# Fourteen modulation blocks beside channel mixing: from narrow TensorE products to sums on VectorE

## The chip, the core and the metric

The kernel runs on one core of one Trainium2 chip. The metric is the device time of one execution in microseconds; the time before is the median of three runs. The engines are named as in the profile: PE is TensorE (PEld its weight loads), DVE is VectorE, ACT is ScalarE, POOL is GpSimd, SP is SyncE, whose queue issues nearly all transfers.

## The reference

Two layers, each with token mixing and channel mixing, run over 512 latent and 256 context tokens of width 1024. Both parts of a layer are modulated: a conditioning vector, one for the latent tokens and one for the context, is multiplied by a large matrix, which gives six rows of 1024 per layer and stream (shift, scale and gate, twice).

```python
sc = silu(c)
sc_ctx = silu(c_ctx)
for l in range(DEPTH):
    last = l == DEPTH - 1
    mod_l = (sc @ w_mod[l] + b_mod[l]).reshape(Bsz, N_MOD, 1, D)
    mod_c = (sc_ctx @ w_mod[l] + b_mod[l]).reshape(N_MOD, 1, 1, D)
    ...
    hl = layer_norm(xl) * (1.0 + mod_l[:, 1]) + mod_l[:, 0]
    ...
    xl = layer_norm(DEEPNORM_ALPHA * xl + mod_l[:, 2] * yl, ln1_g[l], ln1_b[l])
    hl = layer_norm(xl) * (1.0 + mod_l[:, 4]) + mod_l[:, 3]
    xl = layer_norm(DEEPNORM_ALPHA * xl + mod_l[:, 5] * swiglu(hl, w_up[l], w_down[l]), ln2_g[l], ln2_b[l])
    ...
```

Where lines are left out stand the token mixing (RG-LRU scans, spatial gating and Fourier mixing, from which `yl` comes) and the same for the context in layer 0; in layer 1 the context only feeds the scans.

## The kernel before

All large products are done in three passes of a split format: a weight or an activation is kept as a high part (rounded on ACT by a copy) and a low part (the difference, by a subtraction on DVE or POOL), and `mm` multiplies high by high, high by low and low by high. Line 134 is the one place from which every product is issued, and line 203 (`tt`) the one place of plain additions, subtractions and products of two operands, so the profile is read by tile names: `mm` and `aux` are PSUM tiles (three of two banks, two of one bank), `f` and `r` are pieces of one large arena in SBUF, `cst` holds the identity matrix of the transposes.

Weights are "units", listed by `plan` in the order of their use. `pump` reads ahead into free arena space as long as a reserve (`self.reserve`) stays free, on SP's queue; `use` takes the next unit, splits it if it wasn't split, and splits up to `self.ahead` of the units behind it (three in channel mixing).

Token mixing of a layer (`mixing`) follows a string, `STEPS[l]`, one letter a step: `z` a Fourier input projection, `c` the first Fourier product of two token tiles, `p` the preparation of an RG-LRU scan (tanh and exp on ACT), `s` one direction of a scan, `V` and `U` the loading of the gating weights, `v` and `u` the gating projections, `g` a gate projection, `t` the gating, `L` the release of the GELUs, which before it are held back (`self.hold`: the projection is copied out of PSUM, the GELU comes later), `D` the switch of the weights' low halves from POOL to DVE (`wsub`), `m` a modulation block, `R` the gate rows. In this part the order of the products on PE is that of the string.

Channel mixing (`mlp`) runs over 22 blocks of 128 hidden columns in five groups, numbered from 0. A step projects gate and up halves of a block (`up_block`: 96 products in layer 0 and, with 512 columns, 48 in layer 1), multiplies them (L1172 on ACT, L1173 on DVE) and splits the result. At the end of a group, one step late, `project` makes the down products for every token tile, DVE multiplies them with the gate row (L1158) and POOL adds them to the residual.

Beside it the modulation is made, for which `mlp_mods` names a step: blocks 10 and 11 (the gate of channel mixing) of the layer itself at steps 1 and 2, and in layer 0 ten blocks for layer 1 at the steps of `NEXT_AT`: fourteen in all. A block is 512 columns of `w_mod`. `mod_block` makes eight products: the conditioning vectors stand as two columns of a 32-column stationary operand (`stc`), the piece of `w_mod` streams through, and four such products stand side by side in the array. `mod_part` copies the result to SBUF on ACT (L515). One step later it is finished in one of two ways. `mod_put`: four transposes, a short reduction over the four column groups, and the bias, into `modT`. `mod_rows`, for gates: the part is split, and a product with a selector matrix (`sel`) sums the four groups and spreads a row over all partitions, two products per stream, added to the bias rows.

## Time and profile before

| | |
|---|---|
| median of three runs | 1538.25 us (1536.52 to 1541.06) |
| the profiled execution | 1537.34 us |
| its span, first to last instruction | 1535.3 us |
| mean granted clock of TensorE | 0.976 of full |
| PE busy | 1443.5 us, 94% |
| DVE busy | 785.1 us, 51% |
| ACT busy | 553.6 us, 36% |
| POOL busy | 288.0 us, 19% |

Busy is the share of the whole span; the stages differ, so a stretch is read by its own window. "Idle before" is the time in which an engine had nothing to do ahead of an instruction, with the instruction that ended it. In an order of time several instructions of the same kind in a row are merged, with their count behind an x.

Layer 0's channel mixing begins at about 355 us and its last down products end at about 930, where layer 1's first projections are already under way; layer 1's channel mixing begins at about 1167 and runs to the end.

### The profile page before, as it was taken

How to read it: one execution, taken by the hardware profiler on the slowest of the kernel's cores; microseconds unless marked ns; L12 is line 12 of the kernel's file. 1: busy time of each engine (PE TensorE's matmuls, PEld its weight loads, DVE VectorE, ACT ScalarE, POOL GpSimd, SP SyncE). 2: the span in 40 equal slices, each digit the busy share in tenths (PEclk: the TensorE clock that was granted, in tenths of full speed). 3: DMA queues.
4: the chain of work that ended last, by engine and by line, in shares of the span. 5: the costliest groups of instructions: out<-in, count | busy, mean ns of one | idle time of the engine just before them, and what ended most of it. 6: DMA issues, size and time to landing. Idle time of an engine off the chain costs nothing. (4 is left out here: it accounts for less than half of the span.)

```text
span 1535.3 us, 19073 instructions
## 1 busy us (share of the span) xinstructions
PE 1443.5 (94%) x7735; PEld 1195.7 (78%) x7735; DVE 785.1 (51%) x1206; ACT 553.6 (36%) x803; POOL 288.0 (19%) x187
## 2 busy tenths in 40 slices
PE   6999888999999999999999998959898999999997
PEld 3788747788888888888888878757777788888885
DVE  6649857774323322332314386688775452543327
ACT  4576445344202202212203245786535331322210
POOL 3303312230030030030030045212320021020201
PEclk9999999999999999999999999979999999999999
DMA  9403475126106235153117104004518241442101
GB/s 322 136 15 97 131 234 183 38 88 215 42 21 213 68 100 174 55 174 106 52 46 230 41 1 123 15 30 144 176 34 241 83 136 60 127 117 67 57 14 56
DMA packets 169432, 163.59 MB, mean 107 GB/s; under 512 B 10456, under 2 KB 126648, under 8 KB 169344
## 3 DMA queue, kind: packets, MB, share of 16 engines
q1 hardware_dynamic: 169232, 162.08, 33.9%
q8 instruction: 61, 1.00, 0.3%
q0 software_dynamic: 112, 0.30, 0.1%
q14 instruction: 27, 0.22, 0.0%
HBM read 160.25 MB, written 2.10 MB: 106 GB/s over the span
## 5 line engine op out<-in xcount | busy, mean ns | idle before, releaser
L134 PE MATMUL mm<-r,r 128*128 128x512 f32 (+1 forms) x6192 | 1232.6, 360 | 23.0 <-POOL r L203 7.5
L134 PEld LDWEIGHTS mm<-r,r 128*128 128x128 f32 x6192 | 1033.6, 190 | 218.4 <-DVE f L1158 11.7
L208 ACT ACTIVATE r<-f 128x1024 fp32r<-128x1024 f32 (+3 forms) x257 | 227.3, 909 | 611.3 <-PE mm L134 324.3
L203 DVE TENSOR_TENSOR r<-f,r 128x1024 fp32r<-128x1024 f32 (+3 forms) x261 | 270.7, 1065 | 191.0 <-ACT r L208 159.5
L203 POOL TENSOR_TENSOR f<-f,f 128x1024 f32<-128x1024 f32 (+2 forms) x44 | 106.3, 2416 | 681.2 <-DVE f L1158 638.0
L1173 DVE TENSOR_TENSOR f<-mm,f 128x768 f32<-128x768 f32 (+1 forms) x44 | 36.3, 824 | 265.8 <-PE mm L134 259.4
L1158 DVE TENSOR_TENSOR f<-mm,f 128x512 f32<-128x512 f32 (+1 forms) x80 | 76.1, 952 | 158.9 <-PE mm L134 158.6
L203 POOL TENSOR_TENSOR r<-f,r 128x512 fp32r<-128x512 f32 (+2 forms) x56 | 101.5, 1820 | 209.4 <-ACT r L208 142.8
L134 PE MATMUL aux<-r,r 128*128 128x256 f32 (+1 forms) x780 | 109.7, 301 | 24.8 <-DVE r L820 9.9
L134 PEld LDWEIGHTS aux<-r,r 128*128 128x128 f32 x780 | 103.6, 206 | 33.0 <-DVE r L820 12.0
L232 POOL TENSOR_TENSOR smalls<-smalls,neghalf 128x1 f32<-128x1 f32 (+2 forms) x69 | 68.1, 988 | 289.1 <-DVE smalls L231 284.7
L203 DVE TENSOR_TENSOR f<-f,f 128x512 f32<-128x512 f32 (+1 forms) x66 | 60.6, 920 | 11.1 <-ACT f L743 8.3
L1172 ACT ACTIVATE f<-mm 128x768 f32<-128x768 f32 (+1 forms) x44 | 30.6, 696 | 96.2 <-PE mm L134 96.2
L134 PE MATMUL aux<-cst,f 128*128 128x128 f32 (+1 forms) x243 | 37.1, 283 | 24.5 <-DVE f L339 7.3
L601 ACT ACTIVATE f<-aux,modT 128x128 f32<-128x128 f32 x128 | 48.6, 467 | 29.0 <-PE aux L134 29.0
L134 PEld LDWEIGHTS aux<-cst,f 128*128 128x128 f32 (+1 forms) x243 | 28.0, 143 | 36.8 <-ACT f L586 10.2
L586 ACT ACTIVATE f<-f,smalls 128x1024 f32<-128x1024 f32 x19 | 23.6, 1242 | 91.6 <-DVE smalls L585 91.6
L134 PE MATMUL aux<-f,stc 128*32 128x512 f32 x384 | 51.0, 631 | 1.3 <-ACT f L601 1.3
L719 DVE SCALAR_TENSOR_TENSOR f<-mm,par,f 128x255 f32<-128x255 f32 (+3 forms) x48 | 26.1, 606 | 16.2 <-ACT f L713 16.2
L565 DVE BATCH_NORM_STATS2 smalls<-f 128x6 f32<-128x512 f32 x44 | 28.4, 682 | 5.9 <-DMA f<-in_ctx_dram 5.6
L743 ACT ACTIVATE f<-mm,par 128x768 f32<-128x768 f32 x32 | 28.0, 902 | 5.0 <-PE mm L134 3.7
L134 PEld LDWEIGHTS aux<-f,stc 128*32 128x32 f32 x384 | 10.4, 113 | 23.8 <-issue 18.6
(107 smaller groups left out, 612.9 us busy)
## 6 DMA issues: line engine op xcount, KB each, us to landing
f<-in_w_mod_dram SPq DMA_DIRECT2D x96, 512.0 KB
f<-in_w_up_dram SPq DMA_DIRECT2D x88, 512.0 KB
f<-in_w_down_dram SPq DMA_DIRECT2D x40, 512.0 KB
f<-in_w_in_dram SPq DMA_DIRECT2D x28, 512.0 KB
f<-in_w_out_dram SPq DMA_DIRECT2D x16, 512.0 KB
f<-in_b_mod_dram SPq DMA_DIRECT2D x6, 512.0 KB
f<-in_x_dram SPq DMA_DIRECT2D x4, 512.0 KB
f<-in_k_cosl_dram SPq DMA_DIRECT2D x4, 512.0 KB
```

Source lines behind the costliest of these rows:

```text
L134: i = f(*args, **kw)
L203: return eng.tensor_tensor(out=out, in0=a, in1=b, op=op)
L208: i = self.nc.scalar.activation(h, src, AF.Copy)
L232: self.nc.gpsimd.tensor_tensor(out=out, in0=v, in1=self.neghalf[:, 0:n], op=ALU.pow)
L565: nc.vector.bn_stats(out=st[:, c, :], in_=x[:, c * 512 : (c + 1) * 512])
L586: nc.scalar.activation(n.f, x, AF.Identity, bias=nm, scale=r)
L601: nc.scalar.activation(y.f[:, q * P : (q + 1) * P], ps[:, q * P : (q + 1) * P], AF.Identity, bias=self.modT[:, slot, k, s : s + 1], scale= ...
L719: nc.vector.scalar_tensor_tensor(out=o, in0=ps[:, i0 : i0 + o1 - o0], scalar=w(k), in1=o, op0=ALU.mult, op1=ALU.add)
L743: insts.append(nc.scalar.activation(g.f, ps[:, 256:1024], AF.Sigmoid, bias=par[:, col : col + 1]))
L1158: self.nc.vector.tensor_tensor(out=tb.f, in0=ps[:, c], in1=m[:, c], op=ALU.mult)
L1172: nc.scalar.activation(g.f, pg[:, 256 + lo : 1024], AF.Silu)
L1173: nc.vector.tensor_tensor(out=g.f, in0=pu[:, 256 + lo : 1024], in1=g.f, op=ALU.mult)
```

## The change

The fourteen blocks beside channel mixing no longer use `mod_block`. `mod_sum` adds them up on DVE: for each of the eight 128-row pieces of `w_mod`, the conditioning value of that row (a scalar per partition) times the piece, into an accumulator of 128 x 512, one per stream. Each partition then holds a partial sum of its own. `mod_cols` transposes the accumulator on PE (four transposes per stream) and reduces along the free axis on DVE; `mod_gate` splits the accumulator and multiplies it with an all-ones matrix (`onesr`), which sums over partitions and spreads the row. `mod_streams` says how many streams there are: two for layer 0's own blocks and for blocks 0 to 3 of layer 1, one for the rest. A block now spans two steps, two of its four units in each, and the list of loads is in that order. The arena reserve in channel mixing is 6000 columns instead of 5000. Both step strings are changed too: in layer 0 `D` moves from in front of `R` to in front of the last `m`; in layer 1 the first `c` moves ahead of `spp`, and `L` from in front of it to behind `U`. The blocks made inside token mixing stay as they were.

```diff
--- before.py
+++ after.py
@@ -46,7 +46,7 @@
 BETWEEN = 2
 START_RESERVE = 11000
 MIX_RESERVE = (12000, 9000)
-STEPS = ("feaekZeeppzssz6ssgpgpsssVvvsvUuuumgmcLccw7DRmtgmmm", "faeekeeZpsspszzsppLcVcssvsvgUuDsugwgtg")
+STEPS = ("feaekZeeppzssz6ssgpgpsssVvvsvUuuumgmcLccw7RmtgmmDm", "faeekeeZpsspszzcsppVcssvsvgULuDsugwgtg")
 PARAMS_AT = 5
 NEXT_AT = {6: 0, 7: 2, 9: 1, 10: 3, 12: 6, 13: 7, 15: 8, 16: 9, 18: 4, 19: 5}
 
@@ -304,6 +304,7 @@
         nc.vector.memset(self.ones, 1.0)
         self.smalls = cp.tile([P, 24 * 24], F32, tag="smalls", name="smalls")
         self.sel = cp.tile([P, 2, P], F32R, tag="sel", name="sel")
+        self.onesr = cp.tile([P, P], F32R, tag="onesr", name="onesr")
 
         self.Xb = [self.buf(D) for _ in range(NT)]
         self.X = [b.f for b in self.Xb]
@@ -349,6 +350,7 @@
         sl = self.buf(2 * P)
         nc.sync.dma_start(out=sl.f, in_=t["k_sel"])
         nc.vector.tensor_copy(self.sel.rearrange("p s n -> p (s n)"), sl.f)
+        nc.vector.tensor_copy(self.onesr, self.ones)
         sl.free()
 
     def load_tokens(self):
@@ -491,7 +493,12 @@
         at = {1: [(l, 10)], 2: [(l, 11)]}
         if l == 0:
             at.update({f: [(1, blk)] for f, blk in NEXT_AT.items()})
-        return at
+        halves = {}
+        for f, mods in at.items():
+            for m, blk in mods:
+                for i in range(2):
+                    halves.setdefault(f + i, []).append((m, blk, i))
+        return halves
 
     def mod_block(self, l, blk):
 
@@ -546,6 +553,57 @@
             o = out[s][:, hf * 512 : (hf + 1) * 512]
             nc.vector.tensor_tensor(out=o, in0=p2, in1=o, op=ALU.add)
         b.free()
+
+    def mod_streams(self, m, blk):
+
+        return 2 if m == 0 or blk < 4 else 1
+
+    def mod_sum(self, m, blk, q, acc):
+
+        nc = self.nc
+        u = self.use(f"mod{m}.{blk}.{q}")
+        for kk in range(2):
+            k = 2 * q + kk
+            w = u.low.f[:, kk * 512 : (kk + 1) * 512]
+            for s, b in enumerate(acc):
+                c = self.stc[:, k, s : s + 1]
+                if k == 0:
+                    nc.vector.tensor_scalar(out=b.f, in0=w, scalar1=c, scalar2=None, op0=ALU.mult)
+                else:
+                    nc.vector.scalar_tensor_tensor(out=b.f, in0=w, scalar=c, in1=b.f, op0=ALU.mult, op1=ALU.add)
+        self.drop(u)
+
+    def mod_cols(self, m, blk, acc):
+
+        nc = self.nc
+        j, hf = blk // 2, blk % 2
+        slot = {0: 0, 1: 1, 3: 2, 4: 3}[j]
+        red = self.small(8).rearrange("p (s k) -> p s k", k=4)
+        for s, b in enumerate(acc):
+            ps = self.psum_aux()
+            for q in range(4):
+                self.pe.transpose(ps[:, q * P : (q + 1) * P], b.f[:, q * P : (q + 1) * P], self.ident)
+            b.free()
+            nc.vector.tensor_reduce(out=red[:, s, :], in_=ps.rearrange("p (k c) -> p k c", c=P), axis=AX.X, op=ALU.add)
+            nc.vector.scalar_tensor_tensor(
+                out=self.modT[:, slot, hf * 4 : hf * 4 + 4, s], in0=red[:, s, :], scalar=(1.0 if j in (1, 4) else 0.0),
+                in1=self.par[:, j * 8 + hf * 4 : j * 8 + hf * 4 + 4], op0=ALU.add, op1=ALU.add,
+            )
+
+    def mod_gate(self, acc, hf, out):
+
+        nc = self.nc
+        for s, a in enumerate(acc):
+            b = self.buf(1024)
+            h, lo = b.r[:, 0:512], b.r[:, 512:1024]
+            self.split(h, lo, a.f)
+            a.free()
+            p2 = self.psum_aux()
+            self.pe.matmul(p2, self.onesr, h, start=True, stop=False)
+            self.pe.matmul(p2, self.onesr, lo, start=False, stop=True)
+            o = out[s][:, hf * 512 : (hf + 1) * 512]
+            nc.vector.tensor_tensor(out=o, in0=p2, in1=o, op=ALU.add)
+            b.free()
 
     def bcast_row(self, out, src):
         self.nc.sync.dma_start(out=out, in_=src.partition_broadcast(P))
@@ -1181,27 +1239,33 @@
         last = l == DEPTH - 1
         tiles = list(range(NC_T, NT)) if last else list(range(NT))
         lo = 256 if last else 0
-        self.reserve, self.owe, self.ahead, self.weng = 5000, 1, 3, "act"
-        groups, parts, rows = FF_GROUPS, {}, None
+        self.reserve, self.owe, self.ahead, self.weng = 6000, 1, 3, "act"
+        groups, parts, rows, ready = FF_GROUPS, {}, None, []
         m5b, m5 = self.gate_rows(l, 5, not last)
         hq = {}
         nxt = 0
         for gi, (f0, f1) in enumerate(groups):
             while nxt < min(f1 + 1, NFF):
                 hq[nxt] = self.up_block(l, nxt, lo, [first.pop(0) for _ in range(min(2, len(first)))])
-                for m, blk in list(parts):
-                    b = parts.pop((m, blk))
+                for m, blk in ready:
+                    acc = parts.pop((m, blk))
                     if m == l:
-                        self.mod_rows(b, blk % 2, m5, not last)
+                        self.mod_gate(acc, blk % 2, m5)
                     elif blk in (4, 5):
                         rows = rows or self.gate_rows(m, 2, False)
-                        self.mod_rows(b, blk % 2, rows[1], False)
+                        self.mod_gate(acc, blk % 2, rows[1])
                     else:
-                        self.mod_put(m, blk, b)
+                        self.mod_cols(m, blk, acc)
+                ready = []
                 if nxt == PARAMS_AT and not last:
                     self.params(1)
-                for m, blk in self.mlp_mods(l).get(nxt, ()):
-                    parts[m, blk] = self.mod_part(m, blk)
+                for m, blk, i in self.mlp_mods(l).get(nxt, ()):
+                    if i == 0:
+                        parts[m, blk] = [self.buf(512) for _ in range(1 if last else self.mod_streams(m, blk))]
+                    else:
+                        ready.append((m, blk))
+                    for q in (2 * i, 2 * i + 1):
+                        self.mod_sum(m, blk, q, parts[m, blk])
                 nxt += 1
             final = gi == len(groups) - 1
             if final:
@@ -1246,8 +1310,8 @@
         def dma(src, pat, **kw):
             return lambda b: nc.sync.dma_start(out=b.rearrange(pat, **kw), in_=src)
 
-        def mod(l, blk):
-            for q in range(4):
+        def mod(l, blk, qs=range(4)):
+            for q in qs:
                 src = t["w_mod"][l][q * 256 : (q + 1) * 256, blk * 512 : (blk + 1) * 512].rearrange("(k p) n -> p k n", p=P)
                 us.append(Unit(f"mod{l}.{blk}.{q}", 1024, dma(src, "p (k n) -> p k n", n=512), raw=True))
 
@@ -1368,8 +1432,8 @@
                     up(l, nxt)
                     if l == 0 and nxt == PARAMS_AT:
                         params(1)
-                    for m, blk in self.mlp_mods(l).get(nxt, ()):
-                        mod(m, blk)
+                    for m, blk, i in self.mlp_mods(l).get(nxt, ()):
+                        mod(m, blk, (2 * i, 2 * i + 1))
                     nxt += 1
                 down(l, gi, f0, f1)
         self.units = us
```

## Rows read from the trace of the kernel before

**Rows 1.** The page, table of engines: busy us, share of the span, instructions.
```profile
PE 1443.5 (94%) x7735; PEld 1195.7 (78%) x7735; DVE 785.1 (51%) x1206; ACT 553.6 (36%) x803; POOL 288.0 (19%) x187
```

**Rows 2.** Windows: stretch, length, busy PE, PEld, DVE, ACT, POOL (instructions), clock, DMA share.
```profile
384.00:870.00 486.00, 486.00 (x2670) 406.30 (x2669) 144.60 (x165) 98.72 (x116) 59.60 (x26) 1.00 0.34 104
...
1001.70:1021.10 19.40, 3.69 (x14) 2.79 (x13) 18.45 (x23) 19.07 (x25) 0.00 (x0) 0.57 0.13 39
1021.10:1053.00 31.90, 31.77 (x228) 30.51 (x229) 26.25 (x67) 21.76 (x28) 9.91 (x5) 0.94 0.22 68
1200.00:1500.00 300.00, 300.00 (x1325) 248.35 (x1324) 116.66 (x110) 73.26 (x92) 41.74 (x16) 1.00 0.27 81
```

**Rows 3.** Groups of instructions, 384 to 870 us: busy us, mean ns, idle before.
```profile
L134 PE MATMUL mm<-r,r 128*128 128x512 f32 (+1 forms) x2449 | 462.2, 350 | 0.0
...
L203 POOL TENSOR_TENSOR f<-f,f 128x1024 f32<-128x1024 f32 x24 | 58.3, 2429 | 402.4 <-DVE f L1158 395.3 <-DMA f<-in_w_mod_dram 4.2 <-issue 3.0
...
L134 PE MATMUL aux<-f,stc 128*32 128x512 f32 x176 | 21.2, 598 | 0.0
```

**Rows 4.** Order of time, 460 to 560 us, PE's lines: start us, length us, what.
```profile
495.69 1.92 PE L134 MATMUL aux<-f,stc 128*32 128x512 f32 x16
...
497.54 16.96 PE L134 MATMUL mm<-r,r 128*128 128x256 f32 x96
...
514.34 0.60 PE L134 MATMUL aux<-cst,f 128*128 128x128 f32 x4
...
514.87 1.92 PE L134 MATMUL aux<-f,stc 128*32 128x512 f32 x16
...
533.50 0.60 PE L134 MATMUL aux<-cst,f 128*128 128x128 f32 x4
...
533.86 26.36 PE L134 MATMUL mm<-r,r 128*128 128x512 f32 x115
```

**Rows 5.** The chain that ended last, in order of time: start, length, what.
```profile
1165.13 1.91 PE aux L134 x2
...
1167.98 1.17 PE aux L134 x8
...
1183.09 0.99 PE aux L134 x6
...
1195.20 2.32 PE aux L134 x18
```

**Rows 6.** Groups of DVE instructions by form, whole span.
```profile
L203 DVE TENSOR_TENSOR f<-f,f 128x512 f32<-128x512 f32 x45 | 35.1, 782 | 0.7
...
L379 DVE SCALAR_TENSOR_TENSOR f<-f,f 128x512 f32<-128x512 f32 x4 | 2.7, 671 | 0.0
```

**Rows 7.** Order of time, 1034 to 1040 us, POOL and DVE.
```profile
1035.94 2.40 POOL L203 TENSOR_TENSOR r<-f,r 128x1024 fp32r<-128x1024 f32 x1 [9.39 <-ACT r L208]
...
1036.02 2.87 DVE L203 TENSOR_TENSOR f<-f,f 128x512 f32<-128x512 f32 x1
```

**Rows 8.** Order of time, 798 to 832 us, SP's queue, ACT and PE.
```profile
801.79 1.45 SPq L1247 DMA_DIRECT2D f<-in_w_up_dram  x2
...
808.85 1.06 ACT L208 ACTIVATE r<-f 128x1024 fp32r<-128x1024 f32 x1 [42.78 <-DMA f<-in_w_up_dram]
...
823.88 16.96 PE L134 MATMUL mm<-r,r 128*128 128x256 f32 x96
```

**Rows 9.** Order of time, 1012 to 1022 us, PE, ACT and DVE.
```profile
1012.46 1.86 PE L134 MATMUL aux<-r,r 128*128 128x256 f32 x7 [0.46 <-DVE r L820]
...
1019.10 0.69 DVE L203 TENSOR_TENSOR f<-f,f 128x512 f32<-128x512 f32 x1
...
1019.75 1.05 ACT L819 ACTIVATE r<-aux 128x512 fp32r<-128x512 f32 x2
1020.35 1.29 DVE L820 TENSOR_TENSOR r<-aux,r 128x512 fp32r<-128x512 f32 x2 [0.56 <-ACT r L819]
...
1021.10 15.18 PE L134 MATMUL aux<-r,r 128*128 128x256 f32 x108 [6.77 <-DVE r L820]
```

## The prediction, made before the change was run

> **What bounds the kernel now.** The page's table of engines comes first: TensorE (PE) is busy 94% of the span, VectorE (DVE) 51% [rows 1]. That average covers stages with different limits, so the windows come next. In the channel mixing of layer 0 (384 to 870 us) PE is busy 486.00 of 486.00 us at granted clock 1.00 and DVE 144.60; from 1200 to 1500 us, layer 1, it is 300.00 of 300.00 against 116.66 [rows 2]. The groups of instructions of that first window say the same from the other side: the big products had 0.0 us of idle time in front of them [rows 3]. So there every microsecond that leaves PE comes off the end, provided nothing else becomes late, and DVE has 341 us to spare. Layer 1's token mixing is different: from 1001.7 to 1021.1 us PE does 3.69 us of work in 19.40 at a mean clock of 0.57, while DVE and ACT are nearly full [rows 2]. The change edits both kinds of place.
>
> **Part 1: the products that leave PE.** A block is eight products against 32 columns, recorded as 16 instructions, busy 1.92 us. What it costs the stage is start to start. A block behind a projection runs from 495.69 to 497.54, 1.85 us; one behind the four transposes of an earlier block costs more, because those transposes to the next product take 0.36 us without a block (533.50 to 533.86) and 0.53 with one (514.34 to 514.87), so 1.85 + 0.17 = 2.02 [rows 4]. Twelve of the 14 blocks lie in layer 0's channel mixing, half of them behind transposes or the like: 6 x 1.85 + 6 x 2.02 = 23.2 us. In layer 1 the second block is 2.32 us of the chain that ended last, of which I take 1.85 (the rest is two gate products that stay). The first is split in three on that chain, 1.91 + 1.17 + 0.99 us [rows 5]; the 1.91 stands where the last token tile is still being modulated, so without it PE may only wait: 2.2 to 4.1 us, and I take the 2.2. Sum removed: 23.2 + 1.85 + 2.2 = 27.2 us.
>
> **Part 2: what PE gets.** The four layer-1 blocks 0 to 3 keep two accumulators (latent and context), each transposed by itself: eight transposes instead of four, 4 x 0.36 = 1.4 us. The others keep four transposes, and the gate rows keep two products per stream, with the all-ones matrix in place of the selector. Net on PE: 27.2 - 1.4 = 25.8 us.
>
> **Part 3: what DVE gets.** Eight instructions per block and stream over 128 x 512: layer 0's two blocks and layer 1's blocks 0 to 3 have two streams, the other eight one, so 20 x 8 = 160 instructions. No row shows this form with its column scalar; the same operation over 512 SBUF elements with a constant takes 0.67 us, and the additions of that shape average 0.78, waits for GpSimd included [rows 6]. I take 0.69: 160 x 0.69 = 110 us, 99 of it in layer 0 (144 instructions); by the two rows 107 to 125. It goes into 341 us of DVE idle time there, and the 11 us of layer 1 into 183. Twelve full-width reductions replace eight short ones, some 7 us more, hidden likewise. ACT loses 14 evacuations and gains two splits: not on the path. Locally it is tighter. At steps 2, 7 and 10 two half blocks meet: 16 x 0.69 = 11 us, beside DVE's own 144.6 / 486 x 17.0 = 5.1 us in a step of 17.0 us (96 products in 16.96 us [rows 4]). That is 16 of 17; what queues behind the sums is the product of gate and up halves, the low half of that result, and the low halves of weights. The down products of a group need that result one whole step later and weights are split up to three units ahead, so a lag of some microseconds reaches nobody. I cost it at nothing, with up to 8 us for the range.
>
> **GpSimd beside it.** The trace has a DVE addition of 512 elements, two SBUF inputs, that took 2.87 us [rows 7] where another took 0.69 [rows 9]; it ended 0.55 us after a GpSimd subtraction that had started 0.08 us before it. 140 of the 160 new instructions (all but the first of each stream) have two SBUF tensor inputs, and GpSimd's residual additions (2.4 us, 24 of them in layer 0's window [rows 3]) lie in the same stage. If each of the 24 stops a sum for its whole length, DVE loses 24 x 2.43 = 58 us: 145 + 99 + 7 + 58 = 309 of 486. Still covered.
> The Trainium skill (SBUF — State Buffer, § Who interferes with whom) states this as a rule: the engines share one port pair under an exclusive lock, and a VectorE instruction with two SBUF inputs blocks, or is blocked by, a GpSimd instruction that reads SBUF. The row above agrees; by the rule the new sums are the worst kind beside GpSimd work, and the sum changes only if DVE becomes late, which is the second rival.
>
> **Part 4: loads and space.** The w_mod transfers are the same, on SP's queue, but a block's four pieces now come two per step, so at the down products of group 3 two pieces instead of four stand before the weights of step 19. That was the tightest place I found: those weights are issued at 801.79, converted on ACT from 808.85 and used at 823.88 [rows 8], 11 us to spare. Against that, the accumulators hold 512 to 1024 columns (2048 at step 2) and the reserve grows by 1000, about one weight block less read ahead. Nothing either way; a transfer into a freed w_mod buffer now waits for DVE instead of PE, with SP's later loads behind it.
>
> **Part 5: the two step strings.** Layer 0's "D" moves behind three modulation steps: one weight (the last gate column block) has its low half computed on GpSimd instead of DVE: 0, within 1 us. Layer 1 matters more. The first Fourier column step moves from behind the two scan preparations ("p") to directly behind its inputs, and "L", which releases the GELUs, behind the last gate and the loading of u. In the trace PE ends the first column step at 1012.46 + 1.86 = 1014.3, but its evacuation starts on ACT at 1019.75, behind tanh and exp of the preparations, and PE resumes at 1021.10 [rows 9]: 6.8 us. With the evacuation ahead of them PE should resume at about 1015, a gain of 5 to 6.8. After that PE is busy 31.77 of 31.90 us [rows 2], so the gain travels some way; but DVE is busy 18.45 of the 19.40 us and its scans are only put later. Later GELUs save table switches and delay the normalisation before the gating. Bounds: a loss of 2.4 (the scans finish late by the evacuations now ahead of them, 1.05 us on ACT and 1.29 on DVE [rows 9], and nothing is won) to a gain of 9 (the 6.8, and an estimated 2 us for the low clock, 0.57 over the stall [rows 2]). I take 4.
>
> **Sum.** 25.8 + 4 = 29.8 us. The profiled execution is 1537.34 us (span 1535.3), 0.9 below the median of the three timed runs, 1538.25. Forecast on the median: 1538.25 - 29.8 = 1508.5 us, 1.9% less.
>
> **The rivals.**
> First, the step strings give nothing or cost up to 2.4 us while channel mixing gives all: 1538.25 - 25.8 = 1512.5, up to 1514.9. For it: DVE and ACT are nearly full in the stall [rows 2], so the work may only be reordered. Against: the evacuation waits 5.4 us for an engine, not for data. 0.18.
> Second, DVE is late often enough to stop PE in the crowded steps and at the starts of the down groups: a third to two thirds of the gain is given back, 1516 to 1530. For it: 16 of 17 us at three steps, and the GpSimd lock. Against: the average, 52% of the window without the lock. 0.11.
> Third, slower. DVE works in order; a sum whose w_mod piece has not landed, or that GpSimd holds, stands in front of the low halves of the weights, and PE waits for those. There are 28 half blocks; one lock costs 2.87 - 0.69 = 2.18 us; if every one reached PE, 28 x 2.18 = 61 us, and 1508.5 + 61 = 1569.5. It decides from 29.8 / 28 = 1.06 us per half block, not hidden. For it: the 2.87 us row. Against: weights are converted steps ahead, PE had no wait at all in this stage, and the lock can be met only while GpSimd is active, some 60 us of 486. 0.05.
> Fourth, the change moves no time: if PE's seemingly full rows hid another limit of the stage (the loads), the gain would be under 4.6 us, about 1536. DMA is busy 0.34 of the window [rows 2] and the products show no wait for it. 0.03.
>
> **How the numbers follow.** The forecast has 0.63. The range: its fast end is full gain of part 5 and the whole first block of layer 1, 1508.5 - 5 - 1.9 = 1501.6, so 1501; its slow end takes in the first rival and about half of the second, 1522. About 1 or 2 in 10 is left out. A measurement here can tell 0.3%, 4.6 us, from no change: faster takes the forecast and the first two rivals, 0.92; same 0.03; slower 0.05.
>
> **What would show it.** In the profile after: no 32-column products after 384 us (160 records instead of 384); some 160 new DVE instructions of 0.6 to 0.8 us in two new lines, DVE at about 900 us busy; PE still without idle time in channel mixing; a step there of 17 us and the transposes, where a block stood between; the stall before 1021 shorter by some 6 us. Layer 0's channel mixing should be 21 to 23 us shorter. Wrong would be PE idle time behind DVE or ACT in channel mixing, new sums far above 0.8 us, or token mixing of layer 1 longer than before.

## The result, and the profile after the change

The changed kernel takes 1517.6 us (median of four runs, 1516.55 to 1519.18) against 1537.4 for the kernel before in the same comparison: the ratio is 0.987, with an interval of 0.9847 to 0.9895. That is 19.8 us less. The forecast was 29.8 us less, 1508.5; the time lies in the range, near its slow end. It lies in the span of times of the second rival (1516 to 1530), though what that rival names, PE stopped in the crowded steps, is not seen in layer 0's channel mixing (below).

The page of the profile after, its table of engines (busy us, share of the span, instructions), answers to [rows 1]:

```profile
span 1515.3 us, 18862 instructions
...
PE 1417.1 (94%) x7527; PEld 1197.1 (79%) x7527; DVE 896.8 (59%) x1376; ACT 548.2 (36%) x792; POOL 289.8 (19%) x188
```

PE loses 26.4 us of busy time and DVE gains 111.7. The same window as in [rows 2], 384 to 870 us (PE, PEld, DVE, ACT, POOL, clock):

```profile
384.00:870.00 486.00, 486.00 (x2606) 420.90 (x2605) 237.92 (x303) 96.44 (x108) 62.17 (x25) 1.00 0.34 105
```

The groups of DVE instructions by form over the whole span (busy us, mean ns, idle before), for the two new lines and for a line of the first one's form that was there before:

```profile
L573 DVE SCALAR_TENSOR_TENSOR f<-f,stc,f 128x512 f32<-128x512 f32 x140 | 102.4, 764 | 2.2 <-DMA f<-in_w_mod_dram 0.4
...
L571 DVE TENSOR_SCALAR f<-f,stc 128x512 f32<-128x512 f32 x20 | 9.4, 484 | 12.4 <-PE mm L134 9.9 <-POOL f L203 2.3 <-DMA f<-in_w_mod_dram 0.2
...
L678 DVE SCALAR_TENSOR_TENSOR f<-f,smalls,f 128x512 f32<-128x512 f32 x8 | 5.6, 744 | 0.0
```

PE is as full as before, at full clock; the 160 new instructions cost 102.4 + 9.4 = 111.8 us. (Line numbers behind the new functions are some 58 higher than before.)

Where the 20 us went is seen by cutting the span at marks that both traces have. On PE's order of time (start us, length us, what, idle before and what ended it) these are: a, the transposes of the last token tile in layer 0's token mixing; b, the first transposes at the end of its channel mixing; c, the products of the Fourier maps; d, the products with `ones`; e and f, the first and the last transposes at the end of layer 1's token mixing. Before:

```profile
349.82 1.09 PE L134 MATMUL aux<-cst,f 128*128 128x128 f32 x8 [0.78 <-ACT f L586]
...
960.33 1.05 PE L134 MATMUL aux<-f,cst 128*128 128x128 f32 x8
...
1083.13 1.84 PE L134 MATMUL aux<-ones,f 128*128 128x1 f32 x8 [3.24 <-DVE f L203]
...
1129.81 1.09 PE L134 MATMUL aux<-cst,f 128*128 128x128 f32 x8 [0.35 <-ACT f L586]
...
1162.17 0.66 PE L134 MATMUL aux<-cst,f 128*128 128x128 f32 x4 [2.28 <-ACT f L586]
```

and after:

```profile
353.22 1.95 PE L134 MATMUL aux<-cst,f 128*128 128x128 f32 x8 [2.22 <-ACT f L644]
...
879.42 1.09 PE L134 MATMUL aux<-cst,f 128*128 128x128 f32 x8
...
939.97 1.06 PE L134 MATMUL aux<-f,cst 128*128 128x128 f32 x8
...
1061.33 1.02 PE L134 MATMUL aux<-ones,f 128*128 128x1 f32 x8 [2.97 <-DVE f L203]
...
1105.84 1.04 PE L134 MATMUL aux<-cst,f 128*128 128x128 f32 x8
...
1144.48 1.97 PE L134 MATMUL aux<-cst,f 128*128 128x128 f32 x8 [6.60 <-ACT f L644]
```

b was at 897.48 us before. The stretches in us, worked out from these starts, with two experiments told of below (their starts read in the same view):

| stretch | before | after | both old strings | old strings, own sums held |
|---|---|---|---|---|
| start to a: layer 0 token mixing | 349.8 | 353.2 | 353.3 | 352.0 |
| a to b: layer 0 channel mixing | 547.7 | 526.2 | 524.6 | 524.6 |
| b to c | 62.9 | 60.6 | 63.3 | 60.5 |
| c to d: Fourier steps, scans, gating | 122.8 | 121.4 | 118.1 | 117.7 |
| d to e | 46.7 | 44.5 | 46.6 | 46.1 |
| e to f: last token tiles | 32.4 | 38.6 | 35.7 | 31.7 |
| f to the end: layer 1 channel mixing | 373.1 | 370.8 | 369.6 | 369.7 |
| span | 1535.3 | 1515.3 | 1511.2 | 1502.3 |

So layer 0's channel mixing gained 21.5 us, layer 1's 2.3, the three stretches from b to e 5.9 together, and two places lost: the start by 3.4 and e to f by 6.2. From b to f, layer 1's token mixing, it is 265.1 us against 264.7: no gain is left there, and the prediction had named that part growing longer as a sign of being wrong.

These are single executions, and chance is not small in them. A kernel of the experiments below, without the sums of layer 1's own blocks, has the same instructions as the changed kernel in the same order on PE, DVE, ACT and POOL up to 1127 us; its stretches are 354.0, 524.6, 63.2, 122.4 and 45.7 us, so one stretch differs by up to 2.7 us and e comes 4.1 us later. The difference in a to b has a visible source: over the 20 us from a the granted clock was 0.91 in the changed kernel and 1.00 in the other and with the old strings, behind waits of 2.22, 2.26 and 2.23 us. So the verdicts below go by the medians, and a stretch counts only where several traces agree or a wait in it explains the difference.

### The profile page after: what moved, and what is told of

Same layout as the page of the kernel before. It is cut to its first block, busy times and chain, and to the rows that moved or that the text cites. A ratio compares the mean times of both kernels' runs of the same rounds, so it can differ in the third digit from the quotient of the medians.

```text
span 1515.3 us, 18862 instructions
## 1 busy us (share of the span) xinstructions
PE 1417.1 (94%) x7527; PEld 1197.1 (79%) x7527; DVE 896.8 (59%) x1376; ACT 548.2 (36%) x792; POOL 289.8 (19%) x188
## 4 chain that ended last, share of the span: by engine, by line
PE 73%; DVE 13%; ACT 5%; issue 4%; POOL 4%; DMA 2%; SPq 0%; DVEq 0%; POOLq 0%; ACTq 0%
PE mm L134 68%; PE aux L134 5%; POOL smalls L232 2%; DVE r L203 1%; DVE f L203 1%; DVE f L678 1%; POOL r L203 1%; DVE f L1216 1%; ACT r L208 1%; DMA f<-in_b_mod_dram 1%; DVE smalls L709 1%; DVE f L835 1%; DVE f L832 1%; DVE f L1008 1%; DVE f L573 0%
## 5 line engine op out<-in xcount | busy, mean ns | idle before, releaser
L208 ACT ACTIVATE r<-f 128x1024 fp32r<-128x1024 f32 (+3 forms) x259 | 229.1, 907 | 601.6 <-PE mm L134 324.8
L203 DVE TENSOR_TENSOR r<-f,r 128x1024 fp32r<-128x1024 f32 (+4 forms) x262 | 269.7, 1053 | 140.7 <-ACT r L208 116.6
L1216 DVE TENSOR_TENSOR f<-mm,f 128x512 f32<-128x512 f32 (+1 forms) x80 | 76.2, 953 | 150.5 <-PE mm L134 146.8
L573 DVE SCALAR_TENSOR_TENSOR f<-f,stc,f 128x512 f32<-128x512 f32 x140 | 102.4, 764 | 2.2 <-DMA f<-in_w_mod_dram 0.4
L134 PE MATMUL aux<-cst,f 128*128 128x128 f32 (+2 forms) x259 | 39.0, 286 | 29.3 <-ACT f L644 13.4
L134 PEld LDWEIGHTS aux<-cst,f 128*128 128x128 f32 (+2 forms) x259 | 30.6, 145 | 40.4 <-ACT f L644 15.8
L623 DVE BATCH_NORM_STATS2 smalls<-f 128x6 f32<-128x512 f32 x44 | 28.5, 683 | 5.3 <-DMA f<-in_ctx_dram 5.0
L709 DVE BATCH_NORM_STATS2 smalls<-f 128x6 f32<-128x512 f32 x40 | 27.7, 691 | 0.5
```

The costliest lines, as they stand in the source:

```text
L134: i = f(*args, **kw)
L203: return eng.tensor_tensor(out=out, in0=a, in1=b, op=op)
L208: i = self.nc.scalar.activation(h, src, AF.Copy)
L573: nc.vector.scalar_tensor_tensor(out=b.f, in0=w, scalar=c, in1=b.f, op0=ALU.mult, op1=ALU.add)
L623: nc.vector.bn_stats(out=st[:, c, :], in_=x[:, c * 512 : (c + 1) * 512])
L709: nc.vector.bn_stats(out=st[:, hf, :], in_=self.X[ti][:, c])
```

## The experiments

The theory once the two traces had been compared: the products off PE and the sums on DVE do what was forecast in layer 0's channel mixing; what was lost lies in the step strings and at the two starts of channel mixing. Unless a line says otherwise, each is the changed kernel with the edit shown. Two parts of the change were never run alone: the larger reserve and layer 0's `D`.

**Which part gains: the strings or the sums?**

```diff
-STEPS = ("...w7RmtgmmDm", "faeekeeZpsspszzcsppVcssvsvgULuDsugwgtg")
+STEPS = ("...w7DRmtgmmm", "faeekeeZpsspszzsppLcVcssvsvgUuDsugwgtg")
```

> The sums on VectorE with both step strings as before. Theory (channel mixing gives its 21.5 us as forecast; what is missing from the forecast is lost at the two places where channel mixing begins, and the strings are worth +4 us in layer 1 and -2 us in layer 0): the layer 1 gain of the strings goes, the 2 us of layer 0 return, so about 1519.5 us, ratio about 0.988 to 0.989. Rival 1 (the strings are what costs the missing 10 us): 1510 or less, ratio 0.983 or less. Rival 2 (VectorE is late everywhere): ratio unchanged at 0.987, and waits on VectorE inside channel mixing.

1511.6 us (1507.1 to 1513.1), ratio 0.982 (0.9797 to 0.9839): 6 us faster than with the new strings, with intervals apart. The theory was wrong and the first rival nearly right: the strings cost. The opposite edit, the new strings in the kernel before:

> The kernel before with only the two new step strings. Theory: +4 us won in layer 1's token mixing, 2 lost in layer 0's, so about 1535.5 us, ratio 0.998 to 0.999. Rival 1 (the strings cost time): ratio above 1.002. In the trace: PE's stall behind the first Fourier columns is cut in layer 1 but a second one appears behind the second Fourier columns.

1536.4 us, ratio 0.999 (0.9978 to 1.0001). That is as expected: alone the strings gain some 3 us at most, or nothing, and beside the sums they cost 6. A part that does no harm alone can cost time beside another.

**Which letter?** The first Fourier column step alone moved ahead, everything else in the strings as of old:

```diff
-STEPS = ("...w7RmtgmmDm", "faeekeeZpsspszzcsppVcssvsvgULuDsugwgtg")
+STEPS = ("...w7DRmtgmmm", "faeekeeZpsspszzcsppLVcssvsvgUuDsugwgtg")
```

> The sums with the old strings but for one letter: in layer 1 the first Fourier column step stands ahead of the two scan preparations, as in the changed kernel; L and layer 0's D stand where they stood before. With both old strings it is 1511.6 us, with both new ones 1517.6. Theory: the late L is what costs (the burst of gating work behind it makes TensorE wait 4.0 us for a weight's low half at 1042 us), and c alone neither gains nor loses: 1510 to 1513. Rival: c costs (the second column step's evacuation comes behind tanh and exp of the preparations): 1516 to 1519.

1517.7 us, ratio 0.987 (0.9849 to 0.9889): the rival: the column step costs, alone as much as all the letters together. Late L alone:

```diff
-STEPS = ("...w7RmtgmmDm", "faeekeeZpsspszzcsppVcssvsvgULuDsugwgtg")
+STEPS = ("...w7DRmtgmmm", "faeekeeZpsspszzsppcVcssvsvgULuDsugwgtg")
```

> The sums with the old strings but for one letter: in layer 1 L (the release of the GELUs) stands late, as in the changed kernel; the first Fourier column step and layer 0's D stand where they stood before. Both old: 1511.6 us; both new: 1517.6; only the column step moved: 1517.7. Theory: the moved column step is the part that costs (it turns one stall of 6.8 us into two of 1.4 and 6.1, and lowers the clock longer), and a late L costs nothing by itself: 1510 to 1514. Rival: each of the two is enough to spoil the order that was won (an old string with anything moved gives about 1517): 1515 to 1519.

1515.2 us, ratio 0.985 (0.9831 to 0.9873). Again the rival, at its edge: L alone takes some 3.6 us too, with intervals that overlap, so that this is likely and not shown. The column step shows in the order of time. PE in the kernel with both old strings, then PE, ACT and DVE in the changed one (the letter's own lines; others between them left out):

```profile
990.38 1.86 PE L134 MATMUL aux<-r,r 128*128 128x256 f32 x7 [0.46 <-DVE r L878]
999.03 4.29 PE L134 MATMUL aux<-r,r 128*128 128x256 f32 x16 [6.78 <-DVE r L878]
```

```profile
989.15 1.86 PE L134 MATMUL aux<-r,r 128*128 128x256 f32 x7 [0.46 <-DVE r L878]
...
992.38 2.93 PE L134 MATMUL aux<-r,r 128*128 128x256 f32 x12 [1.36 <-DVE r L878]
...
996.50 1.75 ACT L825 ACTIVATE f<-f,spl 128x768 f32<-128x768 f32 x2
...
998.15 1.99 ACT L208 ACTIVATE r<-f 128x1024 fp32r<-128x1024 f32 x2
...
1000.04 1.06 ACT L877 ACTIVATE r<-aux 128x512 fp32r<-128x512 f32 x2
1000.65 1.29 DVE L878 TENSOR_TENSOR r<-aux,r 128x512 fp32r<-128x512 f32 x2 [2.96 <-ACT r L877]
...
1001.40 1.86 PE L134 MATMUL aux<-r,r 128*128 128x256 f32 x7 [6.10 <-DVE r L878]
```

The evacuation of the first column step did come early, as forecast, and PE resumed after 1.36 us. But the second column step, 2.9 us later, then waits 6.10 us for its own evacuation, behind the same tanh and exp and two weight splits (L208). The stall of 6.77 us [rows 9] became two, of 7.46 together. The granted clock from 981.5 to 1001.4 us was 0.50, the lower of the two levels.

This says why the moved step wins nothing, and not why it costs 6 us: the kernel before with the new strings, which was not slower, has both stalls too.

```profile
1014.50 2.93 PE L134 MATMUL aux<-r,r 128*128 128x256 f32 x12 [1.36 <-DVE r L820]
1023.53 13.24 PE L134 MATMUL aux<-r,r 128*128 128x256 f32 x96 [6.10 <-DVE r L820]
```

Beside the sums the traces put the cost further on. From c to e it is 165.9 us in the changed kernel, 168.1 in the run without layer 1's own sums and 168.7 with the column step alone, against 164.7 with both old strings (163.9 and 164.9 in two later runs with them). In e to f it is 38.6 against 35.7, where PE waits 1.50 and 2.20 us for the residuals (L1216) of earlier tiles instead of 0.32 and 0.51. Why the letters do that only beside the sums is open.

**Are the sums hidden?** In one kernel 140 of the 160 sums are left out (all but the first of each stream), in another the 98 such sums of layer 0's ten blocks for layer 1 are made twice (the expectation's "126" should read 112, of which 14 are first products).

```diff
-                else:
+                elif False:
                     nc.vector.scalar_tensor_tensor(out=b.f, in0=w, scalar=c, in1=b.f, op0=ALU.mult, op1=ALU.add)
```

> The changed kernel without 140 of the 160 sums: only the first of the eight pieces of each block and stream is taken, the other seven are left out of the modulation (their transfers stay). Theory (the sums are hidden in channel mixing and cost only at its start): channel mixing of layer 0 as long as with the sums within 1 us, 4 to 6 us less at the start of layer 1's, about 1512.5 us, ratio 0.983 to 0.985. Rival 2: the 102 us of sums press on PE throughout, ratio below 0.980.

```diff
+                    if m == 1 and blk < 10:
+                        nc.vector.scalar_tensor_tensor(out=self.spare.f, in0=w, scalar=c, in1=b.f, op0=ALU.mult, op1=ALU.add)
                     nc.vector.scalar_tensor_tensor(out=b.f, in0=w, scalar=c, in1=b.f, op0=ALU.mult, op1=ALU.add)
```

> The changed kernel with every one of the 126 sums of layer 0's ten blocks for layer 1 made twice, the first time into a spare buffer that nobody reads: 126 - 14 streams' first products = 98 sums of 0.75 us more, some 73 us more of VectorE in layer 0's channel mixing, the same products and transfers. Theory: VectorE is hidden there (238 of 486 us busy), so layer 0's channel mixing stays at 526 us within 2 and the time at 1517.6 within 3. Rival (VectorE late in the crowded steps): at a step in which two blocks of two streams meet, 22 us of sums lie beside 17 us of products, TensorE waits for late halves there, and the time grows by 5 to 20 us.

Without sums 1512.2 us (1510.6 to 1519.9; ratio 0.984, 0.9815 to 0.9866), a to b 526.1. Doubled 1520.4 us (ratio 0.988, 0.9866 to 0.9896), a to b 525.7. The window 384 to 870 us without the sums and with them doubled (PE, PEld, DVE, ACT, POOL, clock):

```profile
384.00:870.00 486.00, 486.00 (x2606) 420.94 (x2605) 161.26 (x195) 95.42 (x107) 60.20 (x25) 1.00 0.34 105
```

```profile
384.00:870.00 486.00, 486.00 (x2607) 421.01 (x2606) 307.10 (x401) 99.07 (x110) 60.45 (x26) 1.00 0.34 104
```

DVE goes from 161 over 238 to 307 us, and PE is full each time: in layer 0's channel mixing the sums cost nothing, and 98 more would not either. Both times are as expected. The 2.8 us by which the doubled kernel is slower are within the intervals; they don't lie in a to b, while c to d took 126.5 us. Why is open.

**What holds the last token tile of layer 1?** The missing sums did gain 5.4 us by the medians, with intervals that overlap. PE's wait at f is 2.08 us without them, 4.5 less, which is the place to look at. (The trace is of the slowest of the four runs, 1519.86 us, so its total says nothing here.) Leaving out only the 14 sums of layer 1's own two blocks:

```diff
-                else:
+                elif not (m == 1 and blk >= 10):
```

> The changed kernel, but of the two blocks of layer 1's own gate only the first product of each accumulator is made; 14 of the 16 sums of that layer are left out (the gate row is then not the reference's), loads, transfers and everything else stay. Theory: these sums stand between the layer-norm statistics of the last token tile (five of 0.75 us from 1131 to 1138 us) and are what makes TensorE wait 6.60 us for the last normalised tile; without them the wait is 2.5 to 3 us and the time 1517.6 - 3.8 = 1513.8 us. Rival: the wait comes from weight splits that are moved ahead with the halved blocks (up weights on ACT and VectorE just ahead of the last normalisation); then it stays above 5 us and the time at 1516 to 1518.

1513.4 us, ratio 0.984 (0.9819 to 0.9859), and the wait is 2.07 us where 2.5 to 3 were expected; the time is as expected. So the long wait is shown to come from these 14 sums, 10 us of DVE; of the time they seem to be 4.2 of the 5.4 us, again with intervals that overlap. In this trace, of the slowest run too (1517.56 us), e to f is 35.7 us, only 2.9 less: the products ahead of f took 13.11 us instead of 11.49, at a granted clock of 0.87 instead of 1.00. DVE's order of time in the changed kernel shows where they stand, between the evacuation of the last tile (L1216) and its final statistics:

```profile
1128.96 0.69 DVE L1216 TENSOR_TENSOR f<-mm,f 128x512 f32<-128x512 f32 x1
1129.56 1.22 DVE L203 TENSOR_TENSOR r<-f,r 128x1024 fp32r<-128x1024 f32 x1
...
1131.29 0.75 DVE L573 SCALAR_TENSOR_TENSOR f<-f,stc,f 128x512 f32<-128x512 f32 x1
1131.95 0.69 DVE L709 BATCH_NORM_STATS2 smalls<-f 128x6 f32<-128x512 f32 x1
1132.62 0.75 DVE L573 SCALAR_TENSOR_TENSOR f<-f,stc,f 128x512 f32<-128x512 f32 x1
1133.29 0.20 DVE L629 BATCH_NORM_AGGREGATE smalls<-smalls 128x2 f32<-128x12 f32 x1
1133.41 0.75 DVE L573 SCALAR_TENSOR_TENSOR f<-f,stc,f 128x512 f32<-128x512 f32 x1
...
1135.94 0.75 DVE L573 SCALAR_TENSOR_TENSOR f<-f,stc,f 128x512 f32<-128x512 f32 x1
...
1137.80 0.75 DVE L573 SCALAR_TENSOR_TENSOR f<-f,stc,f 128x512 f32<-128x512 f32 x1
1138.46 1.28 DVE L623 BATCH_NORM_STATS2 smalls<-f 128x6 f32<-128x512 f32 x2
```

Five sums of 0.75 us each, and the splits of weights beside them, are threaded into a chain in which every step waits for the one before; all sums of the two blocks are done some 40 to 50 us before the gate products at 1188 and 1199 us need them.

One way to move them: both own blocks one step later.

```diff
-        at = {1: [(l, 10)], 2: [(l, 11)]}
+        at = {2: [(l, 10), (l, 11)]}
```

> The changed kernel with the layer's own blocks 10 and 11 both at steps 2 and 3 of channel mixing instead of 1 to 3: their loads and sums come later, away from the layer norms of the last token tiles. Theory (sums stand on VectorE between the statistics of the last tile, and PE waits 6.6 us for it at the start of layer 1's channel mixing where it waited 2.3 before): that wait falls to about 2.3, 4 us less, about 1513.5 us, ratio 0.984 to 0.985. Rival 2 (VectorE is late because it is loaded, wherever the sums are): ratio 0.987 or more.

1526.2 us, ratio 0.992 (0.990 to 0.9935): 8.6 us slower than the change, theory wrong. The wait at f fell only to 5.42 us, and the list of loads, which goes by the steps, moved too: PE waited 7.11 us for a normalised tile at 918.6 us, and c to d took 129.3 us. A step number is not a place on DVE: the first product of these sums, at 1141.59 us, still stands among the last tile's statistics, and what it waited for was the landing of its piece.

Another, with both old strings: the own blocks whole, so that the loads are listed as before the change.

```diff
-                    halves.setdefault(f + i, []).append((m, blk, i))
+                    halves.setdefault(f + (i if f > 2 else 0), []).append((m, blk, i))
```

> The sums with both old strings, and the layer's own two gate blocks again in one step each (four units, eight products of a scalar with a piece per stream), so that their loads are listed as before the change; the ten other blocks stay in halves. Theory: the halved list put weight splits of later steps ahead of the last token tile's statistics; with the old list the stretch from the transposes at 292 us to the last modulation of layer 0's token mixing is 57.2 us again instead of 58.7, the wait for the last normalised tile of layer 1's token mixing is under 4 us instead of 7.0, and the time is 1511.6 - 1.5 - 3 = 1507 us. Rival: the sums themselves stand in the way, and eight at once more than four: the waits stay or grow, 1512 to 1516 us.

1515.9 us, ratio 0.986 (0.9843 to 0.9872), the rival: 4 us slower than with halves. The waits stayed (5.67 us at f), since sums stand there as before, and c to d is 122.8 us, as in the kernel before, instead of 118.1.

A third, with both old strings: the same steps and loads, but the sums made to depend on the modulated last tile, through a copy of their scalars.

```diff
+        z = self.small(4)[:, 0:1]
+        nc.vector.tensor_scalar(out=z, in0=self.XT(NT - 1, NT)[0][:, 0, KC - 1, P - 1 : P].bitcast(F32), scalar1=0.0, scalar2=None, op0=ALU.mult)
+        nc.vector.tensor_scalar(out=self.stg, in0=self.stc[:, :, 0:2], scalar1=z, scalar2=None, op0=ALU.add)
...
-                c = self.stc[:, k, s : s + 1]
+                c = (self.stg if blk >= 10 else self.stc)[:, k, s : s + 1]
```

> The sums with both old strings (1511.6 us), and the scalars of each layer's own two gate blocks are a copy of the conditioning values that is made only when the last token tile has been modulated (its last element times 0 is added), so that no sum of these blocks can stand among the statistics of that tile; the same sums, loads and products. Theory: TensorE's wait for the last normalised tile at the start of layer 1's channel mixing falls from 7.0 to 2 to 3 us, the stretch from the first transposes at the end of that token mixing to the last ones from 35.7 to 31 to 32 us, layer 0's start is as before (weight splits, not sums, stand there), and the time is 1511.6 - 4 = 1507.5 us. Rival: the sums are only put later and are then late for the first group's down products, or weight splits take their place: 1510 to 1514.

1507.1 us (1503.4 to 1509.0), ratio 0.980 (0.9777 to 0.9816), as expected; the interval overlaps a little with that of the sums not held (0.9797 to 0.9839), and the wait and the stretch decide. PE at f:

```profile
1132.62 1.97 PE L134 MATMUL aux<-cst,f 128*128 128x128 f32 x8 [2.91 <-ACT f L645]
```

The wait was 7.01 us, e to f is 31.7 us instead of 35.7, and layer 1's channel mixing is as long as with the sums not held (369.7 and 369.6): the held sums are late for nobody. This version beats both kernels, by 2.0% and by some 10 us.

Is it worth having layer 1's own blocks on DVE at all? With both old strings, these two again as products, whole (the cut lines put back `mod_rows`, the old list of loads and the old reserve for that layer):

```diff
+        if l == 1:
+            return {f: [(m, blk, 9) for m, blk in mods] for f, mods in at.items()}
...
+                    if last:
+                        parts[m, blk] = self.mod_part(m, blk)
+                        ready.append((m, blk))
+                        continue
```

> The sums with both old strings for the twelve blocks of layer 0's channel mixing alone; layer 1's own two blocks are narrow TensorE products again, whole, with the old list of loads and the old reserve there. By the stretches of the traces layer 1's end was 32.4 + 373.1 = 405.5 us before and is 35.7 + 369.6 = 405.3 with its sums and the old strings. Theory: the part of the change that lies in layer 1 brings nothing, because what the sums take off TensorE they give back as a wait for the last token tile: the wait falls back to 2.3 us, the products come back, and the time is 1511.6 within 2 us. Rival (the forecast's own count): those two blocks are worth 1.85 + 2.2 = 4 us, and the time is 1515.6.

1515.5 us, ratio 0.986 (0.9838 to 0.9873): theory wrong, the forecast's count right. Not held, they are worth 3.9 us (the intervals just touch). f to the end is 373.5 us instead of 369.6, the products being back, but the wait at f fell to 4.23 us only: instead of the sums three weight splits of 1.2 us stood among the statistics.

**The start of layer 0's channel mixing.** From the transposes at about 292 us to a it is 57.2 us before (292.60 to 349.82), 58.7 after. Held sums and whole blocks together, with both old strings (the two edits above):

> Both old strings, the own gate blocks' sums held back until the last token tile is modulated (1507.1 us with halved own blocks), and these blocks whole again, one step each, so that their loads are listed as before the change; nothing is left out. Theory for the start of layer 0's channel mixing: two things can stand ahead of the last tile's statistics there, the split of a later weight (with the halved list) and the sums themselves (with the whole list); with both taken away the wait for that tile falls from 2.2 to 0.8 us and the stretch from the transposes at about 292 us to the last modulation is 57.2 us, as before the change; the time is 1507.1 - 1.5 = 1505.6 us, or up to 1511.6 if layer 1's token mixing takes the extra 4 us that it took with the whole list and sums not held. Rival: something else makes the stretch longer; it stays at 58.5 to 58.7.

```profile
348.86 1.09 PE L134 MATMUL aux<-cst,f 128*128 128x128 f32 x8 [0.78 <-ACT f L645]
```

57.2 us again, and the wait is 0.78 us. With halves (also when 140 sums are left out) a weight's split, 1.21 us at 343.12 in the changed kernel, stands ahead of the last tile's statistics; with whole blocks and sums not held, sums stand there. Both had to go. The run with both own blocks one step later, where neither stands there, has 57.2 us and a wait of 0.80 as well. The time, 1514.3 us (ratio 0.985, 0.9827 to 0.9876), is outside what was expected all the same: c to d is 123.4 us, and weight splits make PE wait 4.82 us at f. The rest of the 3.4 us at the start arises before 292 us; two kernels that are equal up to there differ by 1.7 us at that point (294.55 and 296.24), so it may be chance.

## Why the prediction was right, and where it failed

**What bounds, parts 1 and 2: right for layer 0.** 23.2 - 1.4 = 21.8 us were counted for layer 0's channel mixing; a to b is 21.5 us shorter, and 23.0 to 23.1 in six of the other traces, with old and with new strings, where the clock did not fall behind a. PE has 7527 products, as many as counted (7735 - 384 + 160 + 16), and no product with 32 columns is left after 384 us.

**Part 3: right in size and in place, for layer 0.** 110 us were forecast, 111.8 measured: the first product of a stream is cheaper (484 ns) and the sums dearer (748 in the median) than the 0.69 taken. The row that carried the price was there in the trace before, unread, against the prediction's "no row shows this form with its column scalar": the normalisation of half a tile is the same operation, and takes 744 ns after the change too.

```profile
L620 DVE SCALAR_TENSOR_TENSOR f<-f,smalls,f 128x512 f32<-128x512 f32 x8 | 5.6, 744 | 0.0
```

"Costed at nothing" is shown by leaving the sums out and by doubling them, which also settles the second and third rivals for this stage.
GpSimd took far less than the bound of 58 us. The sums' mean is 16 ns above their median, 140 x 0.016 = 2.2 us in all, and one sum makes nearly all of that. It took 2.90 us; it lies with a residual addition that took 3.98 instead of 2.39 us:

```profile
792.85 3.98 POOL L203 TENSOR_TENSOR f<-f,f 128x1024 f32<-128x1024 f32 x1 [4.69 <-DVE f L1216]
793.34 1.23 DVE L203 TENSOR_TENSOR r<-f,r 128x1024 fp32r<-128x1024 f32 x1
...
794.47 2.90 DVE L573 SCALAR_TENSOR_TENSOR f<-f,stc,f 128x512 f32<-128x512 f32 x1
```

The subtraction ends at 794.57; 2.39 us later is 796.96, and the addition ends at 796.83; the sum ends 0.54 us behind it. So the three nearly fit one after another, as by the exclusive lock that the Trainium skill (SBUF — State Buffer, § Who interferes with whom) states. But GpSimd adds during the down products and most sums run beside the projections: of the 24 additions from 384 to 870 us only two, the last of their groups (565.02 and 792.85 us), meet one.

**Part 1, layer 1's own blocks: the size right, the wait not seen.** 1.85 + 2.2 = 4.05 us were counted, and putting the products back cost 3.9 with the old strings. But it was written that at this place "PE may only wait", and the wait was sized by what PE leaves, not by what DVE gets: sums that are ready early stand ahead of the tile's statistics. PE's wait went from 2.28 to 6.60 us, where leaving the sums out or holding them gives 2.07 and 2.91. Part 3 asked who is queued behind the sums and answered for the crowded steps of layer 0; the same question at layer 1's start was not asked. There DVE is on the path: the limit of the place decided, and not the 51% of the span. Held back (in both layers), the sums are 8.4 us faster than the kernel with layer 1's products put back.

**Part 5: failed, and it is the largest miss.** +4 us were taken, with bounds of -2.4 and +9; beside the sums the strings cost 6 us, outside the bounds. The step that failed is "PE should resume at about 1015, a gain of 5 to 6.8": PE did resume, but only to reach the next stall of the same kind 2.9 us later, so that the two stalls were 7.46 us where one was 6.77. The forecast followed one evacuation and not the next user of ACT's queue. The row against it was in the first rival: DVE and ACT nearly full, so that work is only reordered. That accounts for the gain that did not come. The loss lies, as far as the traces tell, in c to e and in e to f, where the forecast allowed for 2.4 us at most; its cause is open. With the old strings the time was 1511.6, where that rival put "the strings give nothing" (1512.5), though not term by term: 1.5 us at layer 0's start and 3.3 in e to f were lost, and c to d gave 4.7 that nobody had counted. So that nearness is in part luck. The place of the changed kernel in the range is luck too: part 5 was 10 us off (from +4 to -6), and the slow end stood at 1522 for the sake of the second rival, whose mechanism did not come about in layer 0.

**Part 4: not nothing.** The order of loads is worth microseconds, by the weight splits that go with it: 1.5 us at layer 0's start, and about 5 in c to d between halved and whole own blocks (118.1 and 122.8 us; held, 117.7 and 123.4), of which the first pair gets 1.9 back in d to e. The sign of this was not foreseen. In the runs with whole blocks a weight's high half, made on ACT, is waited for by 4.1 us in that stretch; how the list brings that about was not followed further, and why each letter costs as much as it does beside the halved list stays open too.

## What to carry to other kernels

Work taken from a full engine is worth its length where that engine is full, and the row of the stage says it within a microsecond or two; where a chain through the receiving engine sets the end, the same work is read again as instructions in that chain's queue. Work with nothing to wait for is done as soon as its data land, not at the step where it is listed: give it a dependence that puts it behind what is urgent. A moved step is followed to the next stall of its kind before its gain is booked, and two edits that come together are run apart.

## What the runs showed of the hardware

The same DVE operation over 128 x 512 fp32 elements takes 748 ns with a column scalar where it took 671 with a constant [rows 6]. Without a second tensor it took 484 with one column scalar, and 766 with two (L410 of the kernel before). A DVE and a GpSimd instruction that meet can both take longer: 0.75 became 2.90 and 2.39 became 3.98 us in one meeting. Of the 24 residual additions from 384 to 870 us 20 kept their 2.39 us, but they met no sum, and two of the other four (3.26 and 3.32 us) are as long when 140 sums are left out. After the 6.60 us wait at f the eight transposes took 1.97 us instead of 1.04; the windows of the changed kernel ahead of, at and behind them (PE, PEld, DVE, ACT, POOL, clock):

```profile
1137.00:1144.40 7.40, 0.88 (x8) 0.68 (x6) 6.96 (x13) 5.72 (x8) 0.86 (x1) 0.82 1.06 290
1144.40:1150.00 5.60, 3.03 (x12) 2.34 (x12) 5.46 (x8) 4.08 (x11) 0.00 (x0) 0.50 0.89 254
1150.00:1160.00 10.00, 10.00 (x64) 10.00 (x65) 4.69 (x6) 4.63 (x5) 0.00 (x0) 0.73 0.51 157
```

PE did 0.88 us of work in the first of them; in the second the clock is at its lower level, and in the third at 0.73 on average although PE is full. By an estimate from these rows 0.50 x 3.03 + 0.27 x 10.00 = 4.2 us at full clock are lost behind the wait. A shorter wait does not save them all: over the 20 us from f the clock was 0.73 here, 0.76 behind the wait of 7.01 us, 0.76 behind that of 2.91 (sums held), 0.83 behind that of 2.07 (without layer 1's own sums) and 0.91 behind that of 2.28 (the kernel before). And the same wait can have a price or none: at a, behind 2.22 us, the transposes took 1.95 us in the changed kernel, and behind 2.23 us 1.09 with the old strings.
